# Transposing and gathering the last adaLN column chunk of the attention stage ahead of the recurrence's loop

## The chip, the cores and the metric

The kernel runs on one core of a Trainium2 chip. The core has a matrix engine (TensorE, PE in the profile, with its weight loads shown as PEld), a vector engine (VectorE, DVE), a scalar engine (ScalarE, ACT), a general engine (GpSimd, POOL) and a queue that issues DMAs (SyncE, SP). Each engine works through its own list of instructions in order, and a semaphore holds an instruction back until what it needs is there. The metric is the device time of one execution in microseconds, lower is better; three runs are made and their median is taken.

## The reference

The reference is one layer of a hybrid diffusion backbone on 1024 latent tokens and 256 context tokens of width 1024. In short:

```python
mod  = split(silu(cond) @ w_ada + b_ada, 6)            # adaLN: shift, scale, gate, twice
h    = rms_norm(x) * (1 + sc1) + sh1
z    = h @ w_in                                         # hq, hf_fwd, hf_bwd, hi, hg, q, k, v, gl
o_a  = attention(rope(rms(q)), [cache_k, rope(rms(k))], [cache_v, v])
o_h  = rms(scan_fwd(...) + scan_bwd(...)) * silu(hg)    # HGRN2 recurrence, 4 heads, chunks of 32
out  = (sig(gl0) * (o_h @ w_ho) + sig(gl1) * (o_a @ w_ao)) @ w_out
x    = x + g1 * out
x    = x + g2 * (relu(mlp_norm(x) @ w_ff1)**2 @ w_ff2)
```

The conditioning product `silu(cond) @ w_ada` has 6 x 1024 columns for two conditionings (latent and context). The kernel makes it in chunks of 256 columns, and one of these chunks is what the change moves.

## The kernel before

Products in fp32 are made from split operands (`hi` rounded, `lo` the rest, three matmuls for each block), so TensorE has much to do, and the kernel fills every wait of one stage with matmuls of another. TensorE's order is the program's order, written by hand (`manual_schedule(engines={PE})`). The order on the other engines is chosen by a planner at compile time, which follows its own cost estimates, priorities (`tc.high_priority(offset=...)`) and edges that the program adds: `tc.issue_after(x)` puts every instruction of its block that runs on x's engine behind x in that engine's list.

**The fillers.** A `Filler` hands out the matmuls of a generator step by step. `with_ada` is that generator: it runs through groups of 256 columns of `w_in` and after each group makes one adaLN chunk by `ada_cols`. The attention stage uses the filler `fz` (groups of the recurrence's inputs, hq to hg), the recurrence uses `fg` (the eight groups `gls` of the branch gates, `gl`). What `fz` has left when attention ends is run out by `fz.rest`, which `hgrn` calls as `before()`.

**An adaLN chunk.** `ada_cols` makes 32 small matmuls into a PSUM bank `pa` of the tag "g" (L176), copies the result to the SBUF tile `ev` on ScalarE (L178), and returns `late`. `late` is kept in the list `todo` and does the rest: a transpose of `ev` on TensorE into another part of the same bank (L182), a sum of the four partial results on VectorE into the tile `adas` (L185, with raised priority; called the gather here), and the addition of the bias into `modc` (L186). The bank is free when L185 has read it. `with_ada` takes a `late` from `todo` and calls it at the seventh step of the next group's first half. The last chunk of `fz` has no next group in `fz`, so its `late` is called by `fg`, at the seventh step of `gls[0]`.

**Banks.** There are three banks of the tag "g", used in turn. Around the change they go to the third, fourth and fifth pair of the last hg group, to the last adaLN chunk, and then to the three token tiles (512, 512 and 256 tokens) of the first half of `gls[0]` (`z_half`, L319 to L321). The first token tile so follows the hg group's fourth pair, the second its fifth pair, and the third the adaLN chunk in their banks. A pair of the hg group is read out by ScalarE (L979) and VectorE (L980); GpSimd multiplies (L982) and SP stores it.

**The recurrence.** `hgrn` has 24 units, one for each head, direction and token tile. `prep` makes a unit's operands: two scans on VectorE (L1008 and L1009 forward, L1012 and L1013 backward), `1 - f` on ScalarE (L1024), a product on GpSimd (L1025), the end-of-block keys on VectorE (L1034, `uf<-usf,um`; kept as `keyed`), the keys of the scores on GpSimd (L1034, `usf<-usf,um`) and the query windows (L1052; L1034, `uw<-uq,um`, one on VectorE and two on GpSimd). `keys_t` transposes the end-of-block keys on TensorE (L1072) and copies them on ScalarE (L1075, kept as `copied`). `scores` is L1083, `states_` is L1095 on TensorE and the chain of L1104 on VectorE, `out` is L1114. In the loop, step i calls `prep` of unit i+1, then scores and states of unit i, the output of unit i-1, and `keys_t` of unit i+1, with matmuls of `fg` between them. `prep` of unit i+1 is queued behind `copied` and `keyed` of unit i on their engines. Units are counted from 0 here, so the second unit is unit 1.

Of the kernel before, what the change touches and what calls it, by code (L numbers as in the profile page):

```python
# [12 lines left out]
ALU = mybir.AluOpType  # L13
AX = mybir.AxisListType
# [30 lines left out]
def build(ctx, tc, I, O, C):  # L45
    nc = tc.nc
    v, s_, g_, pe, sp = nc.vector, nc.scalar, nc.gpsimd, nc.tensor, nc.sync
# [29 lines left out]
    def S(shape=(P, 512), dt=F32, name=None, ring=None):  # L77
        ring = ring or RING_OF[name]
        return (xb if ring == "X" else sb if ring in "DE" else sl).tile(list(shape), dt, tag="s" + ring, name=name, bufs=RINGS[ring])
# [14 lines left out]
    def T(n, name="tiny"):  # L94
        return tp.tile([P, n], F32, tag="tiny%d" % n, name=name, bufs=8 if n <= 16 else 2)
# [7 lines left out]
    def store(out, in_):  # L103
        g_.dma_start(out=f32(out), in_=f32(in_))
# [63 lines left out]
    ones = cp.tile([P, 1], F32, name="ones")  # L168
    v.memset(ones, 1.0)

    def ada_cols(pa, raw, ci):

        for k in range(4):
            for q in range(4):
                kq = 4 * (q // 2) + k
                pe.matmul(pa[32 * q:32 * q + 32, 0:P], ada_l[:, kq, :], raw[:, kq, (q % 2) * P:(q % 2 + 1) * P], start=(k == 0), stop=(k == 3))  # L176
        ev = S((P, P), name="ev")
        s_.activation(ev, pa[:, 0:P], AF.Copy)  # L178

        def late():  # L180
            pt = pa[:, P:2 * P]
            pe.transpose(pt, ev, ident)  # L182
            x = T(4, "adas")
            with tc.high_priority(offset=600):
                v.tensor_reduce(x.rearrange("p (c r) -> p c r", c=2), pt.rearrange("p (i c x) -> p c x i", i=2, c=2)[:, :, 0:2, :], axis=AX.X, op=ALU.add)  # L185
            v.tensor_tensor(modc[:, :, ci:ci + 2], x.rearrange("p (c r) -> p r c", c=2),  # L186
                            cols[:, B_ADA + ci:B_ADA + ci + 2].unsqueeze(1).broadcast_to([P, 2, 2]), op=ALU.add)
        return late
# [166 lines left out]
    class Group:  # L355
# [10 lines left out]
        def part(self, i):  # L366
            if self.w[i] is not None:
                return
            self.load()
            with ExitStack() as after:  # L370
                for x in behind:
                    if x is not None:
                        after.enter_context(tc.issue_after(x.ins))
                self.w[i] = (w_kh if self.tok else w_oc)(self.raw, i)
            if i == 1:
                self.raw = None
# [772 lines left out]
    def hgrn(fill, before):  # L1149

        units = [HUnit(6 * h + j, h, d, t) for h in range(4) for j, (d, t) in enumerate(((0, 0), (0, 1), (1, 1), (1, 0), (0, 2), (1, 2)))]
        fwd = {u.h: {} for u in units}
        for u in units:
            u.fwd = fwd[u.h].get(u.t)
            fwd[u.h][u.t] = u
        N, LATE = len(units), 3

        share = [u.n + 128.0 for u in units] + [300.0] * LATE
        tot, done, st = sum(share), 0.0, None
        with tc.issue_after(gone[0].ins):  # L1160
            units[0].prep()
        before()
        units[0].keys_t()
        for i in range(N + LATE):
            part = lambda x: fill.to((done + x * share[i]) / tot)
            if i + 1 < N:
                with ExitStack() as after:
                    after.enter_context(tc.issue_after(copied[0].ins))
                    after.enter_context(tc.issue_after(keyed[0].ins))
                    units[i + 1].prep()  # L1170
            if i < N:
                u = units[i]
                part(0.25)
                u.scores(u.fwd)
                part(0.5)
                u.states_(u.st or st)
                st = u.last
                if u.t == 2:
                    store(O["new_state_hgrn"][u.d, u.h], st)
                part(0.75)  # L1180
            if i >= LATE and units[i - LATE].d == 1:
                units[i - LATE].out_t()
            if 1 <= i <= N:
                units[i - 1].out(units[i - 1].fwd)
            part(0.95)
            if i + 1 < N:
                units[i + 1].keys_t()
            if 1 <= i <= N and units[i - 1].d == 1:
                units[i - 1].gate(units[i + 1] if i + 1 < N else None)
            part(1.0)  # L1190
            done += share[i]
# [17 lines left out]
    todo = []  # L1209

    def with_ada(groups, b0):

        for i, grp in enumerate(groups):
            nxt = groups[i + 1] if i + 1 < len(groups) else None
            for need, n, gen in grp.stages():
                if not grp.tok and need == (0,):
                    jobs = [(0.5, lambda: grp.part(1))]
                elif nxt:
                    jobs = [(0.05, nxt.load), (0.5, lambda: nxt.part(0))]
                    if nxt.tok and not grp.tok:  # L1220
                        jobs.append((0.75, lambda: nxt.part(1)))
                else:
                    jobs = []
                for j, x in enumerate(gen):
                    if 0 in need and j == 6 and todo:
                        todo.pop()()
                    while jobs and j >= jobs[0][0] * n:
                        jobs.pop(0)[1]()
                    yield x
            if b0 + i < 16:  # L1230
                raw = wraw(I["w_ada"], KC, 2 * D + (b0 + i) * 256)
                ci = 16 + 2 * (b0 + i)
                todo.append(ada_cols(PS("g"), raw, ci))
                yield 1.8
        if todo and b0:
            todo.pop()()
# [10 lines left out]
    with tc.high_priority(offset=600):  # L1247
        gls[0].part(0)
    fg = Filler(with_ada(gls, 10), 194.0)
    hgrn(fg, fz.rest)  # L1250
    fg.rest()
    close("sl")
# [24 lines left out]
    for t in MT:  # L1277
        n = TT[t][1]
        for c in range(8):
            r = S(name="or")  # L1280
# [18 lines left out]
    for c2 in range(4):  # L1299
        r = wp.tile([P, 8, 256], F32, tag="wraw", name="wraw", bufs=2)  # L1300
# [181 lines left out]
    def raw1(i):  # L1482
        return wraw(I["w_ff1"], KC, i * 256)
# [30 lines left out]
    for i in range(NP):  # L1514
        r = raw1(i)
        for half in range(2):
# [6 lines left out]
            if half == 0:  # L1523

                x = pw.tile([P, 4, P], F32, tag="at", name="at", bufs=4)
# [267 lines left out]
    def fw_tile(name):  # L1793
        return xo.tile([P, D], F32, tag="fw", name=name, bufs=1)
# [80 lines left out]
    x = fw_tile("y34")  # L1875
# [85 lines left out]
```

## Time and profile before

| | before |
|---|---|
| median of 3 runs | 2056.77 us (2056.67 to 2057.38) |
| the profiled execution | 2056.44 us |
| its span | 2054.7 us |
| TensorE busy | 98% of the span |
| VectorE, ScalarE, GpSimd busy | 68%, 46%, 26% |
| mean granted TensorE clock | 0.998 |

The span runs from the first to the last instruction that the profiler saw; the execution's own time has 1.74 us around it. A busy TensorE means that matmuls overlap without a gap, not that each runs at full speed. In a list of waits each row says who waited for whom, how long in total, how often and how long at most. In a timeline each row has the start in us from the span's beginning, the duration in us, the engine, the line, the operation with its output and inputs, their shape and the count of merged instructions, and in square brackets the idle time of the engine before it with what ended it.

### The profile page before, as it was taken

The numbers are of one execution on the slowest core, as the hardware profiler recorded it, in microseconds if no ns is written. First come the engines' busy times: TensorE is split into PE (matmuls) and PEld (weight loads), VectorE is DVE, ScalarE is ACT, GpSimd is POOL, SyncE is SP. The second block draws the span as 40 slices with busy tenths as digits, with TensorE's granted clock in tenths as the row PEclk, the third lists the DMA queues.
The fourth block names the chain that finished last, engine by engine and source line by source line (L and its number), as shares of the span: only waits on it lengthen the run. The fifth ranks groups of instructions, "written<-read, shape, count | busy, mean of one in ns | idle before, by whom it ended". The sixth has DMA issues, their size and how long they took to land.

```text
span 2054.7 us, 33792 instructions
## 1 busy us (share of the span) xinstructions
PE 2013.7 (98%) x12470; PEld 1735.2 (84%) x12470; DVE 1407.0 (68%) x2733; ACT 941.1 (46%) x1973; POOL 533.1 (26%) x526
## 2 busy tenths in 40 slices
PE   7899999999999999999999999999999999999998
PEld 5698889988889978888888889988888888888886
DVE  5866776767776788879254635886666666577686
ACT  4634555555555423333321335755455544333443
POOL 1452233333333355545112101222122110000120
PEclk9999999999999999999999999999999999999999
DMA  9452220321212454554644533854444489455764
GB/s 318 160 189 78 70 83 32 104 88 55 77 50 80 132 176 158 165 168 158 199 136 149 179 113 119 253 184 152 159 146 157 145 292 361 147 160 175 232 238 142
DMA packets 220612, 317.38 MB, mean 154 GB/s; under 512 B 18760, under 2 KB 139808, under 8 KB 220448
## 3 DMA queue, kind: packets, MB, share of 16 engines
q1 hardware_dynamic: 207968, 275.32, 41.8%
q0 software_dynamic: 12480, 39.91, 5.2%
q8 instruction: 98, 1.61, 0.3%
q14 instruction: 66, 0.54, 0.1%
HBM read 229.43 MB, written 85.74 MB: 153 GB/s over the span
## 4 chain that ended last, share of the span: by engine, by line
PE 87%; DVE 6%; DMA 3%; ACT 2%; issue 1%; SPq 0%; POOL 0%; POOLq 0%; DVEq 0%; ACTq 0%
PE ps_g L319 8%; PE ps_g L321 7%; PE ps_g L320 7%; PE ps_s L819 4%; PE ps_t L860 4%; PE ps_g L1749 2%; PE ps_g L1748 2%; PE ps_g L1750 2%; PE ps_s L1593 2%; PE ps_s L1594 2%; PE ps_s L1595 2%; PE ps_g L875 2%; PE ps_s L1748 2%; PE ps_s L1749 2%; PE ps_s L1750 2%; PE ps_g L336 2%
## 5 line engine op out<-in xcount | busy, mean ns | idle before, releaser
L319 PE MATMUL ps_g<-hs,wsp 128*128 128x512 f32 (+1 forms) x896 | 322.5, 360 | 4.0 <-DVE adas L185 4.0
L321 PE MATMUL ps_g<-hs,wsp 128*128 128x512 f32 (+1 forms) x896 | 309.6, 345 | 0.0
L320 PE MATMUL ps_g<-hs,wsp 128*128 128x512 f32 (+1 forms) x896 | 309.3, 345 | 0.0
L838 POOL TENSOR_SCALAR pexp<-pexp,rs 128x512 f32<-128x512 f32 (+1 forms) x104 | 169.4, 1635 | 367.0 <-ACT pTh L863 174.4
L286 ACT ACTIVATE wsp<-wraw 128x512 fp32r<-128x512 f32 (+1 forms) x186 | 116.7, 667 | 228.6 <-PE ps_g L320 90.8
L287 DVE TENSOR_TENSOR wsp<-wraw,wsp 128x512 fp32r<-128x512 f32 (+1 forms) x186 | 147.0, 812 | 98.2 <-ACT wsp L286 97.7
L319 PEld LDWEIGHTS ps_g<-hs,wsp 128*128 128x128 f32 x896 | 169.9, 190 | 24.9 <-issue 4.6
L321 PEld LDWEIGHTS ps_g<-hs,wsp 128*128 128x128 f32 x896 | 169.5, 189 | 21.6
L863 ACT ACTIVATE pTh<-ps_t 128x512 fp32r<-128x512 f32 x200 | 118.6, 603 | 143.8 <-PE ps_t L860 142.4
L320 PEld LDWEIGHTS ps_g<-hs,wsp 128*128 128x128 f32 x896 | 170.2, 190 | 15.0
L286 ACT ACTIVATE ah<-ar 128x640 fp32r<-128x640 f32 (+1 forms) x112 | 80.9, 723 | 186.5 <-PE ps_g L1749 102.3
L820 DVE TENSOR_REDUCE mx<-ps_s 128x1 f32<-128x512 f32 (+1 forms) x208 | 137.2, 663 | 41.6 <-PE ps_s L819 40.7
L830 ACT ACTIVATE pexp<-ps_s,ngm 128x512 f32<-128x512 f32 (+1 forms) x208 | 137.5, 670 | 36.0 <-DVE ngm L824 35.2
L863 DVE TENSOR_TENSOR pTl<-ps_t,pTh 128x512 fp32r<-128x512 f32 x200 | 135.4, 680 | 18.0 <-ACT pTh L863 17.8
L287 DVE TENSOR_TENSOR ah<-ar,ah 128x640 fp32r<-128x640 f32 (+1 forms) x112 | 91.9, 821 | 77.0 <-ACT ah L286 75.8
L819 PE MATMUL ps_s<-Kl,Ql 128*128 128x512 f32 (+1 forms) x416 | 131.0, 412 | 1.0 <-ACT pexp L830 0.9
L860 PE MATMUL ps_t<-ident,pexp 128*128 128x128 f32 x800 | 121.4, 273 | 4.3 <-DVE pexp L838 3.0
L336 PE MATMUL ps_g<-wsp,hs 128*128 128x256 f32 x400 | 115.9, 290 | 0.0
L338 PE MATMUL ps_g<-wsp,hs 128*128 128x256 f32 x400 | 112.9, 282 | 0.0
L337 PE MATMUL ps_g<-wsp,hs 128*128 128x256 f32 x400 | 112.6, 281 | 0.0
L875 PE MATMUL ps_g<-pTl,Vl 128*128 128x256 f32 x400 | 105.4, 286 | 3.6 <-DVE pTl L863 3.5
L860 PEld LDWEIGHTS ps_t<-ident,pexp 128*128 128x128 f32 x800 | 93.7, 140 | 16.2 <-DVE pexp L838 4.6
(422 smaller groups left out, 5379.1 us busy)
## 6 DMA issues: line engine op xcount, KB each, us to landing
ar<-AF SPq DMA_DIRECT2D x112, 320.0 KB, 3.3
wraw<-in_w_ff SPq DMA_DIRECT2D x32, 1024.0 KB, 6.2
wr<-in_w_ff SPq DMA_DIRECT2D x128, 256.0 KB, 4.3
wraw<-in_w_in SPq DMA_DIRECT2D x18, 1024.0 KB, 5.6
wraw<-in_w_ada SPq DMA_DIRECT2D x16, 1024.0 KB, 5.7
AF<-a POOLq DMA_DIRECT2D x48, 256.0 KB, 2.8
AF<-t POOLq DMA_DIRECT2D x48, 256.0 KB, 2.3
wa<-in_w_ada SPq DMA_DIRECT2D x32, 256.0 KB, 6.0
```

Source lines behind the costliest of these rows:

```text
L286: s_.activation(hi, raw, AF.Copy)
L287: return v.tensor_tensor(lo, raw, f32(hi), op=ALU.subtract)
L319: pe.matmul(out, hi[:, k, :], mh, start=(first and k == 0), stop=False)
L320: pe.matmul(out, hi[:, k, :], ml, start=False, stop=False)
L321: pe.matmul(out, lo[:, k, :], mh, start=False, stop=(last and k == kcs - 1))
L336: pe.matmul(po[:, bb, :], mh[:, off:off + P], wh[:, k % 4, :], start=(k == 0), stop=False)
L819: pe.matmul(pq[:, 0:n], self.qh[:, q0:q0 + P], K[self.g][var][self.kts[i]], start=(var == 0), stop=(var == 1))
L830: s_.activation(e[:, 0:n], self.ps.pop((j, i))[:, 0:n], AF.Exp, bias=self.mx[j], accum_out=self.sm[j][:, i:i + 1])
L838: NORM[(i + j) % len(NORM)].tensor_scalar(x, x, self.rs[j], None, op0=ALU.mult)
L860: pe.transpose(pt[:, a, j * P:(j + 1) * P], self.Ps[j][i][:, b * P:(b + 1) * P], ident)
L863: behind[:] = s_.activation(hi, pt, AF.Copy), v.tensor_tensor(lo, pt, f32(hi), op=ALU.subtract)
L875: pe.matmul(pv[:, 0:256], V[self.g][kg][:, b, :], lo[:, a, :], start=False, stop=(k == last))
```

## The change

The `late` of the last chunk is called once right after `keys_t` of the first unit and ahead of the loop, so that its transpose stands there in TensorE's order and `fg` finds nothing to call at its seventh step. L185's instruction is kept in `adas[0]`, and in the loop's first step the preparation of unit 1 is put behind it in VectorE's list. Nothing is computed otherwise than before.

```diff
+    adas = [None]
+
     def ada_cols(pa, raw, ci):
...
             with tc.high_priority(offset=600):
-                v.tensor_reduce(x.rearrange("p (c r) -> p c r", c=2), pt.rearrange("p (i c x) -> p c x i", i=2, c=2)[:, :, 0:2, :], axis=AX.X, op=ALU.add)
+                adas[0] = v.tensor_reduce(x.rearrange("p (c r) -> p c r", c=2), pt.rearrange("p (i c x) -> p c x i", i=2, c=2)[:, :, 0:2, :], axis=AX.X, op=ALU.add)
...
         before()
         units[0].keys_t()
+        todo.pop()()
         for i in range(N + LATE):
             part = lambda x: fill.to((done + x * share[i]) / tot)
             if i + 1 < N:
                 with ExitStack() as after:
+                    if i == 0:
+                        after.enter_context(tc.issue_after(adas[0].ins))
                     after.enter_context(tc.issue_after(copied[0].ins))
                     after.enter_context(tc.issue_after(keyed[0].ins))
                     units[i + 1].prep()
```

## Prediction

> **What bounds the kernel now.** I read the page first: engines, and the shares of the chain that ended last.
>
> ```profile
> span 2054.7 us, 33792 instructions
> PE 2013.7 (98%) x12470; PEld 1735.2 (84%) x12470; DVE 1407.0 (68%) x2733; ACT 941.1 (46%) x1973; POOL 533.1 (26%) x526
> PE 87%; DVE 6%; DMA 3%; ACT 2%; issue 1%; SPq 0%; POOL 0%; POOLq 0%; DVEq 0%; ACTq 0%
> ```
>
> TensorE sets the time: what lengthens or shortens its own list moves the end, and the rest only where TensorE waits for it. So the second view is TensorE's waits (who waited for whom: us in total, times, longest).
>
> ```profile
> PE ps_t L259 <- ACT xnb L276: 4.0, 4, 1.4
> PE ps_g L319 <- DVE adas L185: 4.0, 1, 4.0
> ```
>
> The first row is four waits near the kernel's start, none over 1.4 us. The second is one wait of 4.0 us for the gather that the change moves. The timeline shows where it lies.
>
> ```profile
> 719.67 0.66 PE L1072 MATMUL ps_t<-ident,uf 128*128 128x128 f32 x4
> 719.85 0.28 ACT L178 ACTIVATE ev<-ps_g 128x128 f32<-128x128 f32 x1 [0.44 <-PE ps_g L176]
> 720.08 0.48 PE L319 MATMUL ps_g<-hs,wsp 128*128 128x512 f32 x1
> 726.20 0.27 PE L182 MATMUL ps_g<-ident,ev 128*128 128x128 f32 x1
> 733.36 0.39 PE L320 MATMUL ps_g<-hs,wsp 128*128 128x512 f32 x1
> 733.58 0.39 PE L321 MATMUL ps_g<-hs,wsp 128*128 128x512 f32 x1
> 737.72 0.15 DVE L185 TENSOR_REDUCE adas<-ps_g 128x4 f32<-128x8 f32 x1
> 737.92 0.39 PE L319 MATMUL ps_g<-hs,wsp 128*128 128x256 f32 x1 [3.96 <-DVE adas L185]
> 738.83 0.43 PE L1083 MATMUL ps_s<-uw,usf 128*32 128x128 f32 x3
> 742.28 0.28 PE L320 MATMUL ps_g<-hs,wsp 128*128 128x256 f32 x1
> 742.40 0.28 PE L321 MATMUL ps_g<-hs,wsp 128*128 128x256 f32 x1
> 743.59 0.61 PE L1095 MATMUL ps_s<-uv,ukt 128*128 128x128 f32 x4
> ```
>
> The transpose ends at 726.47, the gather starts at 737.72: 11.25 us in which it needed nothing more and stood in VectorE's list behind other work. Meanwhile the second 512-token tile ends, the 256-token tile wants the chunk's bank, and TensorE stops. Its matmuls start 0.22 us apart before the stop (733.36, 733.58), so the next would have started at 733.80; it started at 737.92: **4.1 us**.
>
> The stop has an echo. By stretches (us of the stretch, then PE, PEld, DVE, ACT and POOL busy, granted clock, DMA share, GB/s):
>
> ```profile
> 58.00:64.00 6.00, 3.88 (x25) 2.94 (x23) 5.47 (x19) 6.00 (x20) 0.69 (x1) 1.00 0.19 67
> 738.00:742.00 4.00, 4.00 (x44) 3.36 (x45) 3.96 (x10) 0.00 (x0) 1.60 (x2) 0.59 0.23 87
> 742.00:746.00 4.00, 4.00 (x29) 3.74 (x29) 4.00 (x12) 1.42 (x3) 1.39 (x2) 0.98 0.52 143
> ```
>
> The first row is an early stretch that a rival needs. Behind the stop the granted clock is 0.59 for 4 us and 0.98 for the next 4: 4 x 0.41 + 4 x 0.02 = **1.7 us** of TensorE's work lost. The instructions agree. From 737.92 to 743.59 lie 24 matmuls of 256 columns and 32 score matmuls, 5.67 us. At full clock the former start 0.12 us apart (742.28, 742.40), 2.9 us for 24, and 32 scores take 1.01 us in the chain that ended last:
>
> ```profile
> 752.87 1.01 PE ps_s L1083 x32
> ```
>
> That is 3.9 us, so 1.8 us were lost. I take 1.7. The stop costs 5.8 us, and nearly all of the 1300 us behind it is TensorE's own work, so what is won here should reach the end.
>
> **The change part by part.** *Removed:* 4.1 us of wait and 1.7 us of slow clock, if nothing else is late there. The third token tile's bank is then free from about 720.9, 13 us ahead of its need.
>
> *Moved on TensorE:* the transpose goes from 726.20 to behind the key transposes at 719.67 to 720.08. At its old place it cost a step of 0.1 us. At the new one it meets its operand late: `ev` is ready at 719.85 + 0.28 = 720.13.
>
> ```profile
> L182 PEld LDWEIGHTS ps_g<-ident,ev x16: 137/139/142, 173.8 to 979.6; 128*128 128x128 f32 x16
> 720.36 0.60 ACT L1075 ACTIVATE ukt<-ps_t 128x512 f32<-128x512 f32 x1 [0.23 <-PE ps_t L1072]
> ```
>
> A weight load of 0.14 us and the transpose's step follow, so the next L319 starts near 720.45 instead of 720.08: 0.4 us, less 0.1 saved later, **0.3 us** net. The bounds: 0, if the load overlaps fully; 0.9, if the planner puts the copy of the keys (0.60) ahead of L178 on ScalarE. I take 0.3 because L178 was ahead of that copy here and becomes ready first. The moved step issues no DMA and passes none on SP or GpSimd; the bias addition L186 follows L185 and nobody near waits for it.
>
> *Moved on VectorE, and the wait that is added:* L185 now stands ahead of all of unit 1's preparation. It cannot start before the transpose ends, about 720.7, and ends about 720.9. Unit 1's first scan started at 717.65, so the whole chain behind it starts 3.2 us later.
>
> ```profile
> 717.65 1.57 DVE L1008 TENSOR_TENSOR_SCAN ucp<-R,uf 128x512 f32<-128x512 f32 x1
> 718.81 0.60 ACT L979 ACTIVATE ze<-ps_g 128x512 f32<-128x512 f32 x1 [0.45 <-issue]
> 719.15 2.23 DVE L1009 TENSOR_TENSOR_SCAN usf<-uf,R 128x511 f32<-128x511 f32 x1
> 721.41 0.72 ACT L1024 ACTIVATE uf<-uf,ones 128x512 f32<-128x512 f32 x1 [0.45 <-DVE usf L1009]
> 722.48 3.10 POOL L1034 TENSOR_TENSOR uw<-uq,um 128x512 f32<-128x512 f32 x2 [2.09 <-DVE um L1028]
> 725.52 0.68 DVE L287 TENSOR_TENSOR wsp<-wraw,wsp 128x512 fp32r<-128x512 f32 x1
> 726.12 0.68 DVE L980 SCALAR_TENSOR_TENSOR ze<-ze,ps_g 128x512 f32<-128x512 f32 x1
> 726.87 1.28 POOL L982 TENSOR_TENSOR ze<-ze,hnb 128x512 f32<-128x512 f32 x1 [1.30 <-DVE ze L980]
> 727.12 0.48 PE L319 MATMUL ps_g<-hs,wsp 128*128 128x512 f32 x1
> 728.11 1.29 POOL L1025 TENSOR_TENSOR usf<-uf,usf 128x512 f32<-128x512 f32 x1
> 729.44 0.69 DVE L1034 TENSOR_TENSOR uf<-usf,um 128x512 f32<-128x512 f32 x1 [2.65 <-POOL usf L1025]
> 730.21 1.90 POOL L1034 TENSOR_TENSOR usf<-usf,um 128x512 f32<-128x512 f32 x1 [0.80 <-DVE uf L1034]
> 731.30 0.60 PE L1072 MATMUL ps_t<-ident,uf 128*128 128x128 f32 x4
> ```
>
> What is queued behind is unit 1's preparation; who waits for it is TensorE's key transpose of unit 1 (731.30, now 731.6) and its scores (738.83, now 734.8). The reader is to see that the old chain was not tight: L1025 had its input at 722.13 but ran at 728.11, because GpSimd's list had the two window products and L982 ahead of it, and L982 waited for the hg group's last eviction L980, which VectorE's list had only at 726.12. VectorE idled 2.65 us for it.
>
> Now VectorE has a hole from 717.7 to 720.7, and ready for it are L980 (its operand, L979's output, came at 719.4) and the two weight splits L287, the second of which had run at 725.52. L980 becomes ready ahead of L178's copy on ScalarE and so ahead of L185; I take it to go into the hole. Then L982 is out of the way early, and unit 1's keys need 720.9 + 3.7 (scans) + 0.8 (L1024) + 1.3 (L1025) + 0.7 (L1034) = 727.4. If GpSimd still does the window products first, they run 3.2 us later, to 728.8, and the keys come at 728.8 + 1.3 + 0.7 = 730.8. TensorE wants them at 731.6, so the cover is 0.8 to 4.2 us. The scores' keys need another 2.0 us: 732.8 at the latest against 734.8. I cost the delay at **nothing**; without that cover it would be 1 to 3 us.
>
> *What is late next:* TensorE comes 5.5 us earlier to everything behind. The nearest needs:
>
> ```profile
> 739.93 0.73 DVE L1104 SCALAR_TENSOR_TENSOR ust<-ust,udec,ps_s 128x128 f32<-128x128 f32 x2
> 740.58 0.68 DVE L1034 TENSOR_TENSOR uf<-usf,um 128x512 f32<-128x512 f32 x1
> 747.24 0.39 PE L1114 MATMUL ps_s<-s,uw 128*128 128x128 f32 x2
> 749.52 0.60 PE L1072 MATMUL ps_t<-ident,uf 128*128 128x128 f32 x4
> ```
>
> Unit 0's states were ready at 740.66 and are now wanted at 741.7; unit 2's keys were ready at 741.26, now wanted at 744.0. If VectorE kept its hours the cover would be 1.0 us. It starts 3.2 us late but has 3 x 0.6 us of L980 and splits behind it already, and up to 2.65 us of idle to give back, so the states end between 739.4 and 742.1. That is 0 to 0.4 us of wait, taken as 0. From there on each preparation is released by `copied`, so it follows TensorE's shift.
>
> **The sum**, against the profiled execution: 2056.44 - 4.1 - 1.7 + 0.3 = 2050.9. The median stands 0.33 above that execution, so 2051.3 in the median's terms. By bounds: 2050.9 with the transpose free and 1.8 for the clock; 2052.3 with the dearest transpose (0.6 more) and the states late by 0.4. The three runs of before lie 0.7 apart, so I put 0.4 or 0.5 around both: 2050.4 to 2052.7.
>
> **The rivals.**
>
> *Unit 0's states or unit 2's keys late.* If the hole stays empty and VectorE's 2.65 us of idle comes back as well, the states end at 743.8, 2.1 us past their need. For it: the cover of 1.0 us above. Against it: L980 and two splits are ready for the hole. Gain left 5.5 - 2.1 = 3.4, less what clock is lost: 2053.4 to 2055.1.
>
> *The hg eviction is late.* The second token tile's bank waits for L980: 726.80 against 727.12, only 0.3 us apart. If L980 stays behind unit 1's preparation, 8.5 us behind the first scan as now, it ends at 720.9 + 8.5 + 0.7 = 730.1 and TensorE stops for 2.6 us at 727.5. The clock's price for that lies between nothing (the wait of 1.4 us lies in the stretch from 58 to 64, whose clock is 1.00) and 1.7 (the wait of 4.0). Gain left 1.2 to 2.9: 2053.9 to 2055.6, no change by the bound below. Against it: the order of readiness above. [...]
>
> *The same eviction behind unit 2's scans* is the case on the other side. L185 itself stood there, 20 us behind unit 1's first scan. L980 would end near 720.9 + 20.1 - 2.7 + 0.7 = 739, TensorE would stop at 727.5 for 11.5 us and lose 1.7 more: 5.5 - 13.2, 2064.5. It decides from an eviction that ends at 731.3 (stop and slow clock then eat 5.5 us), and is slower by over 0.2% from 735.4. For it: the gather had just this fate. Against it: L980 precedes unit 1 in the program, and the added edge holds back what overtook it.
>
> *The gather moves and something else holds the same tile*, a bank's eviction on ScalarE for instance: the time stays near 2056.8. Against it: the wait names L185 alone, and the bank's last reader is L185.
>
> **How the numbers follow.** About 0.2%, 4.1 us, is what a measurement of this kernel can tell from no change: faster means below 2052.7, slower above 2060.9. The forecast (2050.4 to 2052.7) has 0.72, late states or keys 0.09, the late eviction 0.09, the slower case 0.05, no effect 0.05. The range goes from 2050.4 to 2054.6: the forecast, most of late states and some of the late eviction, a little over 0.8. Faster 0.72, slower 0.05, the same 0.23.
>
> **What would show it.** L182 right behind L1072 on TensorE, a pause there of at most 0.5 us; L185 near 720.7 and L1008 behind it; L980 between L1008's old place and L185; no row of TensorE waiting for L185; granted clock 1.00 in every stretch from 720 to 760; unit 1's L1072 without a wait near 731.6; L1114 of unit 0 near 741.7. Wrong would be a wait of L319 for L980 near 727.5, of L1072 for L1034, or of L1114 for L1104, or new waits further on, if the planner's order shifts in later units.

## The result and the profile after

| | before | after |
|---|---|---|
| median | 2057.40 us (14 runs, 2055.89 to 2059.85) | 2052.07 us (14 runs, 2051.20 to 2057.49) |
| the profiled execution | 2056.44 us | 2053.12 us |
| its span | 2054.7 us | 2051.2 us |
| mean granted TensorE clock | 0.998 | 0.999 |

The changed kernel takes 0.9977 of the time before (95% interval 0.9968 to 0.9985): 5.3 us less as the medians stand, 3.1 to 6.6 us by the interval. The median of before is now that of 14 runs; the first three had given 2056.77. In the new file the lines stand two further down: L184 is the transpose, L187 the gather, L982 the hg eviction, L1074, L1097, L1106 and L1116 are the key transposes, the states on TensorE, their chain on VectorE and the output.

The waits of TensorE in the changed kernel, as shown before: nobody waits for the gather any more, the row of L261 is as it was, and the recurrence has one new row.

```profile
PE ps_t L261 <- ACT xnb L278: 4.0, 4, 1.4
PE ps_s L1097 <- issue: 0.7, 1, 0.7
```

The same stretch of the timeline, TensorE first. Unit 0's key transposes stand at 719.99 here and at 719.67 before, so times are compared from there.

```profile
719.99 0.66 PE L1074 MATMUL ps_t<-ident,uf 128*128 128x128 f32 x4
720.18 0.28 ACT L180 ACTIVATE ev<-ps_g 128x128 f32<-128x128 f32 x1 [0.44 <-POOL ze L984]
720.51 0.33 PE L184 MATMUL ps_g<-ident,ev 128*128 128x128 f32 x1
720.59 0.48 PE L321 MATMUL ps_g<-hs,wsp 128*128 128x512 f32 x1
731.71 0.60 PE L1074 MATMUL ps_t<-ident,uf 128*128 128x128 f32 x4
734.24 0.28 PE L321 MATMUL ps_g<-hs,wsp 128*128 128x256 f32 x1
741.94 0.39 PE L1116 MATMUL ps_s<-s,uw 128*128 128x128 f32 x2
744.22 0.60 PE L1074 MATMUL ps_t<-ident,uf 128*128 128x128 f32 x4
752.27 1.13 PE L1097 MATMUL ps_s<-uv,ukt 128*128 128x128 f32 x8 [0.73 <-issue]
```

The reader is to see that the 256-token tile now starts at 734.24 without a stop, where it stood for 3.96 us. Unit 0's output comes 21.95 us behind the first key transposes (27.57 before) and unit 2's key transposes 24.23 us behind them (29.85 before): 5.62 us are won up to there. The last row is the new pause. From VectorE's list in the same time:

```profile
717.38 0.69 DVE L982 SCALAR_TENSOR_TENSOR ze<-ze,ps_g 128x512 f32<-128x512 f32 x1
718.20 2.52 DVE L289 TENSOR_TENSOR wsp<-wraw,wsp 128x512 fp32r<-128x512 f32 x2
720.63 0.68 DVE L982 SCALAR_TENSOR_TENSOR ze<-ze,ps_g 128x512 f32<-128x512 f32 x1
721.23 0.15 DVE L187 TENSOR_REDUCE adas<-ps_g 128x4 f32<-128x8 f32 x1
721.31 1.21 DVE L1010 TENSOR_TENSOR_SCAN ucp<-R,uf 128x512 f32<-128x512 f32 x1
...
730.08 0.68 DVE L1036 TENSOR_TENSOR uf<-usf,um 128x512 f32<-128x512 f32 x1
...
735.64 0.34 DVE L1106 SCALAR_TENSOR_TENSOR ust<-ust,udec,ps_s 128x128 f32<-128x128 f32 x1
...
740.87 0.69 DVE L1036 TENSOR_TENSOR uf<-usf,um 128x512 f32<-128x512 f32 x1 [1.19 <-POOL usf L1027]
741.48 1.22 DVE L1014 TENSOR_TENSOR_SCAN ucp<-R,uf 128x512 f32<-128x512 f32 x1
...
747.77 0.33 DVE L1106 SCALAR_TENSOR_TENSOR ust<-ust,udec,ps_s 128x128 f32<-128x128 f32 x1
...
751.07 1.10 DVE L1106 SCALAR_TENSOR_TENSOR ust<-ust,udec,ps_s 128x128 f32<-128x128 f32 x3
```

Two weight splits and the last hg eviction fill the hole ahead of the gather, and unit 1's first scan follows it. The chain that ends at 752.17 is unit 1's states; the matmuls of unit 2's states start 0.10 us later, at 752.27. And the clock, by stretches as before:

```profile
732.00:736.00 4.00, 4.00 (x50) 3.31 (x48) 3.93 (x10) 0.85 (x2) 0.11 (x1) 1.00 0.87 257
736.00:740.00 4.00, 4.00 (x35) 3.83 (x31) 3.65 (x10) 2.38 (x5) 2.99 (x3) 1.00 0.41 135
748.00:752.00 4.00, 3.55 (x36) 2.51 (x25) 3.93 (x7) 0.00 (x0) 2.52 (x2) 1.00 0.33 80
```

The slow stretch is gone. Of the stretches shown only the one in which the pause begins has TensorE idle.

**Where the whole gain lies.** Two profiled executions differ outside the recurrence too: the first key transposes start anywhere from 719.4 to 722.0 in the kernels below, and two executions of the changed kernel spent 1050.8 and 1049.5 us behind the recurrence. So the recurrence is measured by itself, from the first key transposes to the start of the last output transpose. That is the last start in this row (count, then minimum, median and maximum in ns, then first and last start), of before and of after:

```profile
L1144 PE MATMUL ps_t<-ident,uo x10: 270/272/273, 992.7 to 1004.9; 128*128 128x128 f32 x10
```

```profile
L1146 PE MATMUL ps_t<-ident,uo x10: 270/272/273, 988.2 to 1000.3; 128*128 128x128 f32 x10
```

Before: 1004.9 - 719.7 = 285.2 us. After: 1000.3 - 720.0 = 280.3 us. So 4.9 us are won in the recurrence, though 5.62 had been won by 744. This length is called the recurrence's length below. Unit 3's key transposes show what the pause takes back (before, then after):

```profile
762.33 0.60 PE L1072 MATMUL ps_t<-ident,uf 128*128 128x128 f32 x4
758.02 0.60 PE L1074 MATMUL ps_t<-ident,uf 128*128 128x128 f32 x4
```

They come 42.66 us behind the first key transposes before and 38.03 after, so only 4.63 us are left: the pause costs 1.0 us, not only the 0.73 that its row shows as idle. Near the recurrence's end, at 946 in the kernel before, another 0.26 us is won; what the kernel before loses there stays open.

### The profile page after: what moved, and what is told of

Same layout as the page of the kernel before. It is cut to its first block, busy times and chain, and to the rows that moved or that the text cites. A ratio compares the mean times of both kernels' runs of the same rounds, so it can differ in the third digit from the quotient of the medians.

```text
span 2051.2 us, 33788 instructions
## 1 busy us (share of the span) xinstructions
PE 2011.8 (98%) x12470; PEld 1734.3 (85%) x12470; DVE 1409.7 (69%) x2733; ACT 941.4 (46%) x1973; POOL 534.2 (26%) x526
## 3 DMA queue, kind: packets, MB, share of 16 engines
q8 instruction: 98, 1.61, 0.3%
## 4 chain that ended last, share of the span: by engine, by line
PE 87%; DVE 5%; DMA 3%; ACT 2%; issue 1%; SPq 1%; POOL 0%; POOLq 0%; DVEq 0%; ACTq 0%
PE ps_g L321 8%; PE ps_g L323 7%; PE ps_g L322 7%; PE ps_s L821 4%; PE ps_t L862 4%; PE ps_g L1755 2%; PE ps_g L1753 2%; PE ps_g L1754 2%; PE ps_s L1598 2%; PE ps_s L1600 2%; PE ps_s L1599 2%; PE ps_g L877 2%; PE ps_g L338 2%; PE ps_g L340 2%; PE ps_g L339 2%; PE ps_g L876 2%
```

## The experiments

Two questions are open: which part of the change wins the time, and what the new pause is. A third came up with the forecast's terms: what a wait of TensorE costs in clock. The texts on record use letters for theories. A says that only the gather's place in VectorE's list counts, ahead of unit 2's scans; B says that the added edge, or in the second experiment the early transpose, is what helps; D says that the pause is the bank that unit 1's late states still hold; H is a guess of the author's, that every stop of more than 2 us costs as much slow clock as the 4.0 us stop of before did, 1.7 us.

**The transposition without the edge** (the changed kernel less these lines):

```diff
-                    if i == 0:
-                        after.enter_context(tc.issue_after(adas[0].ins))
```

> The transpose stands behind the first unit's key transposes as in the changed kernel, but nothing queues unit 1's preparation behind the gather. The compiled order puts the gather on VectorE behind unit 1's query window and the last hg eviction, ahead of unit 2's scans. Theory A (only the place ahead of unit 2's scans and the two weight splits counts; the bank is wanted at 734): the gather runs near 727, TensorE does not wait for it, the clock stays at 1.00, and the time is the changed kernel's or up to 0.7 us less, 2051.4 to 2052.4, ratio to before 0.997 to 0.998. Theory B (the added edge is what helps): the gather comes too late, a wait for it stays, 2055 to 2057. The last hg eviction runs near 726.5, so the second token tile's bank is just free at 727.5.

Measured: 2052.07 us (before 2056.92; ratio 0.998, 0.9971 to 0.9989), recurrence 280.3 us. VectorE's timeline of this kernel:

```profile
728.41 0.68 DVE L982 SCALAR_TENSOR_TENSOR ze<-ze,ps_g 128x512 f32<-128x512 f32 x1
729.01 0.15 DVE L187 TENSOR_REDUCE adas<-ps_g 128x4 f32<-128x8 f32 x1
731.72 0.69 DVE L1036 TENSOR_TENSOR uf<-usf,um 128x512 f32<-128x512 f32 x1 [1.26 <-POOL usf L1027]
```

The gather falls behind much of unit 1's preparation, 7.0 us after unit 0's key transposes (722.0 here) instead of 1.2, and that is early enough: TensorE has no stop but the pause of 0.69 us. The added edge is not needed, as theory A has it; with the transpose early, the planner places the gather ahead of its need without the edge.

**The edge without the transposition**, put where it can hold back only unit 2's preparation (the changed kernel with this edit):

```diff
-        todo.pop()()
...
-                    if i == 0:
+                    if i == 1:
```

> The transpose stays at its old place in TensorE's list (726); only unit 2's preparation, not unit 1's, is queued behind the gather. Theory A: the gather runs near 731 behind unit 1's keys, 3 us ahead of the bank's need; no wait, clock 1.00, and TensorE does not pay the 0.2 us pause for the early transpose: 2051.2 to 2052.2. Theory B (the transpose has to come early): a wait for the gather stays, 2055 to 2057. Rival C (unit 2's preparation, now later, becomes the wait): unit 2's keys or unit 0's states are named in TensorE's waits, 2052.5 to 2055.

Measured: 2052.62 us (ratio 0.9979, 0.9971 to 0.9988), recurrence 281.0 us. The gather was expected near 731 and ran at 735.07, behind two weight splits that waited for ScalarE. TensorE had no stop there all the same (the third token tile started at 735.34), the clock was 1.00 in every stretch, and the pause grew to 1.42 us. An order on VectorE, with the transpose at its old place, so wins all but 0.7 us of the recurrence's 4.9. The median lies 0.4 us above theory A's range and in rival C's; the late states are unit 1's, though, and not unit 0's.

**A bank of its own for this chunk's transpose**, nothing moved (the kernel before, with this edit; `own` is set for this chunk only):

```diff
-            pt = pa[:, P:2 * P]
+            pt = PS("t")[:, 0:P] if own else pa[:, P:2 * P]
```

> Nothing is moved: the kernel before, but this one chunk's transpose goes into a bank of the tag t instead of the spare part of the chunk's g bank, so the g bank is free once ScalarE has copied it at 720.1. Bank theory: the gather still runs near 737.7 and nobody waits; the stop of 4.1 us and 1.7 us of slow clock both go, VectorE's order stays that of before; unit 0's states at 740.7 against a need at 741.5, unit 1's states at 751.0 against 750.9: gain 5.4 to 5.8, 2051.2 to 2052.2. Rival (the early gather frees VectorE's list for what TensorE needs next): the wait moves to the states or the keys and at most 3 us are gained, 2054 or more.

Measured: 2052.02 us (ratio 0.9977, 0.9969 to 0.9986), recurrence 280.4 us. Three rows of its timeline:

```profile
733.57 0.28 PE L319 MATMUL ps_g<-hs,wsp 128*128 128x256 f32 x1
737.49 0.15 DVE L185 TENSOR_REDUCE adas<-ps_t 128x4 f32<-128x8 f32 x1
751.75 1.13 PE L1095 MATMUL ps_s<-uv,ukt 128*128 128x128 f32 x8 [0.87 <-issue]
```

The gather is as late as ever and the third token tile starts 3.9 us ahead of it. TensorE did not need the gathered values here; it waited only for the bank from which they are read. The pause stands here too (0.87 us), with nothing moved on VectorE.

**Unit 1's states ahead of unit 3's preparation** (the changed kernel and this; `stated` is the last L1106 of a unit):

```diff
+                    if i == 2:
+                        after.enter_context(tc.issue_after(units[1].stated.ins))
```

> The changed kernel, and unit 3's preparation is also queued behind unit 1's chain of states on VectorE. In the changed kernel's trace the weight loads of unit 2's L1097 wait from 748.2 to 752.2, and the chain L1106 of unit 1, which reads the bank that L1097 writes, ends at 752.17: TensorE stands for 0.73 us that the profile puts down to nothing. Theory D (that bank, held by the late states, is this wait): the pause of 0.73 goes, the states end near 743, 2051.0 to 2051.7. Rival E (instruction fetch or chance): the pause stays or shows elsewhere, 2052.1 as the changed kernel. Rival F: unit 3's keys come too late at 757 and take the gain back.

```profile
744.57 1.10 DVE L1106 SCALAR_TENSOR_TENSOR ust<-ust,udec,ps_s 128x128 f32<-128x128 f32 x3
745.58 1.22 DVE L1014 TENSOR_TENSOR_SCAN ucp<-R,uf 128x512 f32<-128x512 f32 x1
751.92 1.05 PE L1097 MATMUL ps_s<-uv,ukt 128*128 128x128 f32 x8
```

Unit 1's states end at 745.67 (expected near 743), 6.5 us earlier than in the changed kernel, unit 3's scans stand behind them, and L1097 of unit 2 no longer pauses. The recurrence takes 279.4 us; to the hundredth it is 279.36 against 280.33 in the changed kernel, 1.0 less. Theory D holds. The median is 2051.17 us (ratio 0.9975, 0.9966 to 0.9984): whether this 1.0 us is won in the whole time can't be told from intervals of this width.

**The preparation later still.** To measure the cover of unit 1's keys, reductions were added between the gather and that preparation, four in one kernel and eight in the other. They are work that the reference doesn't ask for.

```diff
+        with tc.issue_after(adas[0].ins):
+            for k in range(4):
+                late_by = v.tensor_reduce(T(1, "late_by"), R, axis=AX.X, op=ALU.max)
...
-                        after.enter_context(tc.issue_after(adas[0].ins))
+                        after.enter_context(tc.issue_after(late_by.ins))
```

> The changed kernel with 4 more reductions of 128x512 on VectorE (about 0.6 us each, results unused) between the gather and unit 1's preparation, so that the preparation starts 2.4 us later still; the compiled order also puts two weight splits, a score mask and two state steps (2.4 us together) ahead of unit 1's keys. In the changed kernel's trace these keys end at 730.77 and TensorE takes them at 731.71: cover 0.94. Theory (the added wait is free only within this cover): keys near 735.6, TensorE stops about 3.9 us at unit 1's key transposes, with or without 1.7 us of slow clock: 2055.5 to 2058. Rival (unit 1's preparation is not what TensorE is near to waiting for): no stop there, 2052 to 2053.

> The same with 8 reductions: keys near 738.2, a stop of about 6.5 us at unit 1's key transposes and the clock at half for 3.4 us behind it: 2059.5 to 2061, slower than the kernel before by 2 to 4 us though the gather stays early. Rival: no stop, 2052 to 2053.

The keys of unit 1, and TensorE's transposes of them, with four and then with eight:

```profile
734.05 0.68 DVE L1036 TENSOR_TENSOR uf<-usf,um 128x512 f32<-128x512 f32 x1
734.79 0.66 PE L1074 MATMUL ps_t<-ident,uf 128*128 128x128 f32 x4 [1.67 <-DVE uf L1036]
```

```profile
734.74 0.68 DVE L1036 TENSOR_TENSOR uf<-usf,um 128x512 f32<-128x512 f32 x1
735.47 0.66 PE L1074 MATMUL ps_t<-ident,uf 128*128 128x128 f32 x4 [4.00 <-DVE uf L1036]
```

Counted from unit 0's key transposes (721.2, 719.6 and, in the changed kernel, 720.0) the keys are ready 13.5, 15.8 and 10.8 us later. Four reductions so delay them by 2.7 us and cost a stop of 1.67; eight delay them by 5.0 and cost 4.00. The difference is 1.0 both times: that is the cover. The times were 2053.14 us (ratio 0.9983, 0.9974 to 0.9992) and 2057.55 us (1.0005, 0.9995 to 1.0014), the recurrences 281.2 and 285.1 us. The stop of 4.00 brought a slow stretch with it (a granted clock of 0.50 from 736.27 to 739.68) and ate the gain; the stop of 1.67 brought none (1.00 in each 4 us from 728 to 744). Both stops were expected longer (3.9 and 6.5 us). The reductions did add in full: unit 1's first scan starts 2.4 and 4.8 us later than in the changed kernel, counted as above. What did not add is the other 2.4 us of the expectation, for two weight splits, a mask and two state steps that now stand ahead of the keys: from that scan's start to the keys it takes 9.7 us in both kernels, against 9.45 in the changed one.

**Stops of several lengths.** Twelve stops of 1.65 to 4.11 us were made in TensorE's list, each at full load around it, by a transpose that needs a chain of copies on ScalarE. They too add work (an edit of the changed kernel; `stop` is called in twelve of the loop's steps, with 2 to 6 for `n`).

```diff
+        def stop(n):
+            po = PS("g")
+            for k in range(4):
+                pe.transpose(po[:, k * P:(k + 1) * P], ident, ident)
+            e = S((P, P), name="ev")
+            with tc.high_priority(offset=2000):
+                for k in range(n):
+                    s_.activation(po, po, AF.Copy)
+                s_.activation(e, po[:, 0:P], AF.Copy)
+            pe.transpose(po[:, 0:P], e, ident)
```

> The changed kernel with twelve made stops of TensorE in the recurrence: four transposes of the identity, 2 to 6 copies of their bank on ScalarE, one copy to SBUF, and a transpose of that, whose result is unused. Stops of about 1.7 (2 copies, twice), 2.3 (3, twice), 2.8 (4, three times), 3.4 (5, three times) and 3.9 us (6, twice), some 34 us in all. [...] Rival H (any stop over 2 us costs its 1.7): half clock behind ten of the twelve, 2100 or more.

Its one execution took 2107.84 us, in the range of H. Yet H does not fit the trace: it asked for half clock behind ten of the twelve stops, and it came behind seven (granted clock 0.50). Length alone does not sort these stops: of two stops of 2.27 us one was followed by half clock and one was not, and of three stops of 2.82 us one was and two were not. The half-clock stretches behind the stops start at 768.41, 819.61, 836.68, 870.81, 908.36, 942.49 and 993.69; the steps between these are 15, 5, 10, 11, 10 and 15 times 3.413 us. So the trace was read in windows of that grid (columns as in the stretches above). In turn: a stop of 2.27 us almost whole in one window, a stop of 2.82 across two, another of 2.82 with 2.74 us in one, the other of 2.27 with its larger part in the window shown, and the second and third window of the longest stop, 4.11 us.

```profile
765.00:768.41 3.41, 1.30 (x10) 1.26 (x11) 2.17 (x5) 1.97 (x4) 2.13 (x3) 1.00 0.33 108
768.41:771.83 3.42, 3.42 (x10) 2.53 (x9) 1.36 (x4) 0.00 (x0) 0.00 (x0) 0.50 0.00 0
...
778.65:782.07 3.42, 2.21 (x18) 1.54 (x10) 3.42 (x11) 1.14 (x2) 2.36 (x3) 1.00 0.20 77
782.07:785.48 3.41, 1.80 (x13) 1.68 (x14) 2.76 (x11) 1.76 (x5) 1.64 (x2) 1.00 0.24 69
785.48:788.89 3.41, 3.41 (x32) 3.41 (x31) 0.90 (x2) 0.30 (x1) 1.49 (x2) 1.00 0.47 122
...
867.40:870.81 3.41, 0.67 (x8) 0.42 (x4) 3.41 (x13) 3.16 (x8) 0.00 (x0) 1.00 0.69 214
870.81:874.22 3.41, 3.34 (x13) 3.05 (x14) 3.24 (x8) 0.02 (x1) 2.00 (x2) 0.50 0.79 261
...
922.01:925.42 3.41, 1.55 (x12) 1.46 (x13) 3.00 (x12) 1.72 (x4) 2.23 (x3) 1.00 0.90 308
925.42:928.84 3.42, 3.42 (x22) 2.95 (x21) 1.11 (x4) 0.38 (x1) 0.60 (x2) 1.00 0.02 5
...
836.68:840.09 3.41, 1.76 (x9) 1.77 (x9) 0.00 (x0) 1.50 (x4) 0.00 (x0) 0.50 0.14 43
840.09:843.50 3.41, 3.41 (x17) 3.41 (x17) 1.39 (x4) 0.00 (x0) 0.00 (x0) 0.50 0.00 0
```

Around these stops each window in which TensorE was idle for 2.11 us or more (765.00: 3.41 - 1.30) was followed by one at half clock; behind those with 1.86 us or less (922.01: 3.41 - 1.55) the clock stayed at 1.00, but for one. So the stop of 2.82 us that two windows share, with 1.21 us of idleness in the one and 1.61 in the other, lost no clock. The exception is the last pair: a window that was itself at half clock and had 1.65 us of idleness was followed by another. Early in the kernel, among short transposes, half clock followed as much idleness in a window at full clock too (the kernel with unit 1's states ahead, in its second execution):

```profile
77.08:80.49 3.41, 1.76 (x12) 1.16 (x11) 3.41 (x8) 1.75 (x4) 2.45 (x3) 1.00 0.38 126
80.49:83.90 3.41, 3.41 (x10) 2.63 (x9) 3.41 (x4) 0.89 (x2) 2.36 (x2) 0.50 0.16 54
```

At nearly the same place the kernel before had 1.63 us of idleness in a window (76.57 to 79.98) and the changed kernel 1.61 (77.70 to 81.11), and the clock stayed at 1.00 behind both. Six windows, five around the twelve stops and the one from 77.08, had 1.65 to 1.86 us of idleness, and half clock followed two of them. What else decides there stays open.

The stop of the kernel before, with its own grid:

```profile
735.34:738.75 3.41, 0.82 (x6) 0.76 (x6) 3.41 (x6) 0.00 (x0) 3.41 (x3) 1.00 1.08 361
738.75:742.17 3.42, 3.42 (x41) 2.84 (x40) 3.38 (x9) 0.00 (x0) 1.02 (x2) 0.50 0.05 18
```

Of this stop 2.59 us fell in one window, and the next, at half clock, lost 3.42 x 0.5 = 1.7 us.

**The own bank and the states together:** the two edits above on the kernel before.

> Parts of two earlier runs together: the kernel before with this chunk's transpose in a t bank (no move of the transpose or the gather), and unit 3's preparation queued behind unit 1's chain of states. Theory: no stop, no slow clock, no early pause at the transpose (0.2 us) and no pause at unit 2's L1095 (0.87 us in the run with the own bank alone): 2050.7 to 2051.3, up to 0.4 us under the changed kernel with the states ahead (2051.17). Rival: VectorE's list of before makes unit 0's states or unit 3's keys late instead, 2051.5 to 2052.5.

Measured: 2052.02 us (ratio 0.9977, 0.9968 to 0.9985), no stop of TensorE and a clock of 1.00 from 716 to 760, recurrence 279.3 us. The stops went as expected; the median came out 0.7 us above the range expected.

**The three best once more, on one chip:** the changed kernel, the one with unit 1's states ahead, and the one with the own bank and the states.

> The changed kernel once more, beside the next two on one chip. By the traces so far its recurrence (first key transposes to the last output transpose on TensorE) takes 280.3 us against 285.2 before: 4.9 less. Its median should stand 4.5 to 5.5 under that of before, and the pause of about 0.7 us ahead of unit 2's L1097 should be there again if it is a matter of order and not of chance.

> The changed kernel with unit 3's preparation behind unit 1's states, on the same chip: recurrence 279.4 us, no pause at unit 2's L1097, median 0.5 to 1.2 us under the changed kernel's. If it stands within 0.3 of it, the win of 0.7 is given back behind the recurrence.

> The kernel before with the chunk's transpose in a t bank and unit 3's preparation behind unit 1's states, on the same chip: recurrence 279.3 us, median as the run with the states ahead, 0.5 to 1.3 us under the changed kernel's. Its first median (2052.0) was another chip's; if it stands above the changed kernel here too, the order of before costs something behind the recurrence.

| | median, first and second time | second ratio | recurrence, first and second time |
|---|---|---|---|
| changed kernel | 2052.07, 2052.67 us | 0.9975 (0.9965 to 0.9985) | 280.3, 280.3 us |
| states ahead | 2051.17, 2052.51 us | 0.9971 (0.9961 to 0.998) | 279.4, 279.4 us |
| own bank, states ahead | 2052.02, 2051.45 us | 0.997 (0.9959 to 0.9981) | 279.3, 279.3 us |

The recurrence's length repeats to 0.1 us, and it is 1 us shorter with the states ahead. The pause of the changed kernel came again (0.7 us), so it belongs to the order and not to chance. The medians were expected 0.5 to 1.3 us under the changed kernel's; that with the own bank is 1.2 under it, that with the states ahead only 0.2, and its profiled execution spent 1051.0 us behind the recurrence against 1049.5. In the whole time the intervals overlap, and no version is shown to beat the changed kernel there.

## Why the prediction was right, and where it was off

The forecast was a gain of 5.5 us; the medians give 5.3, the recurrence 4.9. The time, 2052.07, lies 0.8 us above the 2051.3 forecast and inside the forecast's own range. That the medians come so close to 5.5 is in part luck: their interval is 3.1 to 6.6 us, and the forecast left out a term of 1.0 us (the step that failed, below). Line numbers in this section are those of the kernel before.

- **The wait (4.1) and the slow clock (1.7): right.** Both are gone, and 5.62 us are won by unit 0's output and unit 2's keys, where 5.5 were forecast. That the wait was the bank's is shown by the kernel with the own bank; that the slow clock follows the stop, by the kernel with eight reductions, where both came back together.
- **The early transpose (0.3): right in kind.** `ev` came at 720.46, the transpose at 720.51, and the first filler matmul stands 0.60 us behind the key transposes instead of 0.41: 0.2 us, less the 0.1 saved at the old place.
- **The hole on VectorE: right.** The splits and the last L980 filled it, the eviction being 6.2 us ahead of the second token tile (727.53 by the 0.48-us matmul that starts it). Neither eviction rival took place.
- **The delay of unit 1's preparation at nothing: right, with the smallest cover named.** The first scan starts 3.3 us later against the key transposes (forecast 3.2). The keys are ready at 730.76 and used at 731.71; the two kernels with reductions give 1.0 us of cover, and 0.8 was the lower end. The reason was another than the one given for that end: the window products did not stand ahead of L1025 on GpSimd here (it ran at 725.53, they at 726.82). The keys waited behind a query window, L1028 and a split in VectorE's list.
- **Unit 0's states and unit 2's keys: no wait, as forecast,** but with far more room for the former: they end at 735.98 for a need at 741.94, where 739.4 to 742.1 was forecast.
- **The step that failed: "From there on each preparation is released by `copied`, so it follows TensorE's shift."** `copied` is an instruction of ScalarE and holds back only what a preparation runs there; the scans are VectorE's and stand behind `keyed`. Unit 3's first scan ran right behind unit 2's keys (740.87) and ahead of unit 2's key transposes (744.22), whose copy `copied` is. So TensorE came 5.6 us earlier and VectorE did not: that scan ran at 741.48, and before at 741.18. From the kernel before:

```profile
741.18 1.22 DVE L1012 TENSOR_TENSOR_SCAN ucp<-R,uf 128x512 f32<-128x512 f32 x1
749.93 1.10 DVE L1104 SCALAR_TENSOR_TENSOR ust<-ust,udec,ps_s 128x128 f32<-128x128 f32 x3
756.66 1.05 PE L1095 MATMUL ps_s<-uv,ukt 128*128 128x128 f32 x8
```

In the kernel before, unit 1's states ended at 751.03, 5.6 us ahead of the matmuls of unit 2's states. That room was the cover. After, the states end at 752.17, and TensorE stands idle for those matmuls from 751.54. They wait because scores, states and outputs take three banks in turn, and unit 2's states get the bank that unit 1's chain still reads. VectorE is the full engine there (in the changed kernel busy for 19.55 of the 20 us from 720 to 740 and 18.92 of the next 20), so what it does late stays late. The pause does not hang on the moved gather: the kernel with the own bank, whose VectorE runs in the order of before, ends unit 1's states at 751.65 and pauses for 0.87 us. The rival "unit 0's states or unit 2's keys late" had this mechanism, at one unit too early and at 2.1 us instead of 1.0.

- **The clock's price in the eviction rival** was bounded by the lengths of two stops, 1.4 and 4.0 us. Length is not what decided in the runs: the made stops nearest to the rival's 2.6 us, of 2.27 and 2.82 us, lost no clock where one window of the grid held at most 1.86 us of them, and had one window at half clock behind them, 3.41 x 0.5 = 1.7 us, where it held 2.11 or 2.74. By the author's estimate from these, a stop of 2.6 us could have cost either.

The sum that stands in the traces is 5.62 - 1.0 for the pause + 0.26 won near the end = 4.9 us, the recurrence's gain. The 0.4 us from there to the 5.3 of the medians are within their scatter.

## What to carry to other kernels

When TensorE waits for a small instruction on another engine, ask first whether it needs the result or only the bank in which it lies; an own bank, an earlier operand and an order on the other engine are then three ways to the same gain, and here each gave it, the last all but 0.7 us. When an engine is relieved of a wait, compare the times of its next few needs with those of the engine that feeds it: here the feeder, full with work, kept its times, and a reserve of 5.6 us behind the edit turned into a pause. Measure such an edit in the stretch that it touches, between two instructions that both kernels have, since the whole time scatters by as much as the remaining microsecond.

## What the runs showed of the hardware

The half-clock stretches lay on a grid: all seven behind the made stops began at whole multiples of 3.413 us from one another, and each lasted 3.41 us or twice that. Nine windows had 2.11 us or more without a matmul, seven around the made stops, one in the kernel before (2.59 us) and one in the kernel with eight reductions (2.61 us, 732.86 to 735.47), and half clock followed all nine; of six windows with 1.65 to 1.86 us it followed two. The stops of 2.27 and 2.82 us lost no clock where one window held at most 1.86 us of them and, by the half-clock window behind them, another 1.7 us where it held 2.11 or 2.74.

A wait for a bank was labelled "issue" in the profile: the pause of 0.73 us ended 0.10 us behind the last instruction that read the bank (752.17 and 752.27). It stood as close behind it in three other kernels (751.65 and 751.75 with the own bank, 754.16 and 754.3 without the edge, 754.01 and 754.1 with the edge alone), and went when that instruction was put ahead (745.67, in the kernel with the states ahead).
